# Loading a recurrent state by 32 by 32 blocks and finishing its transpose on VectorE

## The chip, the cores and the metric

The kernel runs on one core of a Trainium2 chip. The metric is the device time of one execution in microseconds (us). The program is unrolled: there is no loop on the chip, and each engine works through its own list of instructions in order. The engines are PE (TensorE), DVE (VectorE), ACT (ScalarE), POOL (GpSimd) and SP (SyncE, which here only issues DMAs); DMAs run on 16 DMA engines that all queues share.

## The reference

One layer of a hybrid decoder serves one prompt of 256 tokens and eight samples of eight tokens each, 320 tokens in all, in fp32. A combined projection feeds two recurrent branches. The branch that matters here is RWKV-7, with 16 heads of 64 by 64 state, indexed [value, key]:

```python
def step(s, inp):
    r_t, w_t, k_t, v_t, kk_t, a_t = inp
    sa = jnp.einsum('nhvk,nhk->nhv', s, kk_t)
    s = (s * w_t[:, :, None, :]
         - sa[..., None] * (kk_t * a_t)[:, :, None, :]
         + v_t[..., None] * k_t[:, :, None, :])
    return s, jnp.einsum('nhvk,nhk->nhv', s, r_t)
```

The prompt starts from a zero state. Each sample starts from a given state, `state_rwkv` (layers, samples, heads, value, key), and returns the new one. Both products with the old state sum over the key. The other branch, HGRN2, has eight heads and a state indexed [key, value]. After both, three more projections and a final norm follow.

## The kernel before

**Stages.** A start (to about 27 us) normalizes and transposes the tokens. Then a recorded part, to about 650 us, computes the projection in column blocks of 128 and both recurrences, for eight head pairs p of the RWKV branch (two heads at a time) beside the eight heads of the other. The last part, to the end, does the remaining projections. Weights come in blocks of 512 KB (`raw`); ScalarE rounds each to `whi`, VectorE subtracts to get the rest `wlo`, and TensorE multiplies both parts with the tokens (`hhi`, `hlo`) into `mps`. There are three buffers each of `raw`, `whi` and `wlo`.

**The recorder.** In the recorded part every call goes through `Recorder` (line 79): `V`, `S`, `G`, `T` and `Y` are proxies of VectorE, ScalarE, GpSimd, TensorE and SP. `add` (line 97) notes each operation with a cost and its tiles; a DMA on SP costs 380 ns and lands 5500 ns later in this plan, or 4500 to 6500 through scratch memory (line 169). `link` finds the dependencies and gives each operation a rank, the length of the longest chain behind it. `order` then simulates the engines and writes out the order in which each gets its instructions. `choose` (line 338) picks the next operation of an engine among those that can start within `AHEAD` = 300 ns of the earliest; `worth` (line 377) ranks them. On SP, an operation that belongs to no weight block has worth 3, a weight load whose block TensorE needs within 4500 ns has 2, and any other weight load 0. Nothing is reordered after that: an instruction that has to wait holds up everything behind it on its engine. In the profile all operations that are emitted this way carry line 199.

**The head pair.** `rwkv(p, ...)` (line 912) does one head pair. It asks for the two small matrices `w2a2` and for the samples' states of its two heads, in one DMA, as `s0` (line 923): 128 partitions (head, value) by 8 samples by 64 keys, 256 KB. The products with the old state need the key on the partitions. So four TensorE transposes with the identity turn `s0`, two samples at a time, into a PSUM bank `ps0`, and one ScalarE copy brings that to SBUF as `s0t` (lines 990 to 995): partition 64 x (sample mod 2) + key, then the sample's pair, then (head, value). `s0t` has one buffer. It is read by the matmuls with `az` (line 1140), which are part of a group that TensorE does side by side with the other branch's work, and by those with `rz` (line 1262), near the end of the head pair. `s0` itself is scaled and added to in place (line 1223), and stored as the new state (line 1241); it too has one buffer, so the next head pair's load waits for that store.

`at(name, shape)` gives a tile from a ring of `bufs` buffers (one unless told otherwise); `aps(name)` borrows one of six PSUM banks; `quads` are the four groups of 32 partitions. In the profile's names trailing digits are left out, so `s0` and the other branch's state of the same name are both `s`, and PSUM tiles of the recorded part are `bank`; `bank<-ident,s` are the four transposes of `s0`.

Of the kernel before, what the change touches and what calls it, by code (L numbers as in the profile page):

```python
# [20 lines left out]
NSEQ = 8  # L21
# [27 lines left out]

class Op:  # L50
    __slots__ = ("eng", "fn", "args", "kw", "cost", "lat", "uses", "mode", "passes", "cols", "stream",
                 "loans", "succ", "npred", "ready", "rank", "block", "margin", "wait", "port", "hold", "dma", "n", "group")


def span_of(ap):
# [23 lines left out]
class Recorder:  # L79
# [17 lines left out]
    def add(self, eng, name, fn, args, kw):  # L97
        o = Op()
        a, k = args, kw
        o.eng, o.fn, o.args, o.kw, o.n = eng, fn, args, kw, len(self.ops)  # L100
        aps = [x for x in (*args, *kw.values()) if hasattr(x, "start_partition") or hasattr(x, "tensor")]
        out = aps[0]
# [4 lines left out]
        for j, x in enumerate(aps):  # L107
            t_ = x.tensor
            if t_.name.startswith("bank"):
                n, off = divmod(x.offset, LOAN)  # L110
# [6 lines left out]
            o.uses.append((*self.spans[key], j == 0, "PSUM" in str(x.space)))  # L117
        o.lat = self.LAT[eng]
        o.dma = "dma" in name
        o.mode = None  # L120
        o.block, o.group = self.block, self.group
        o.margin, o.wait = 0, self.wait
# [4 lines left out]
        if eng == "PE":  # L127
# [4 lines left out]
            n = 1  # L132
# [39 lines left out]
        if eng in self.DRAIN and not o.dma:  # L172
            o.cost += self.SPARE
            if name == "tensor_reduce":
                n = 1
# [79 lines left out]
    def order(self):  # L255
# [4 lines left out]
        ready = {e: [] for e in self.real}  # L260
# [5 lines left out]
        port = {"V": 0.0, "G": 0.0}  # L266
        bigs = [o for o in self.ops if o.eng == "PE" and o.stream]
        at = {}
# [48 lines left out]
        def entry(q, now):  # L317

            at_, asking = {}, {}
            for o in q:  # L320
                want = wanted(o)
                if not want:
                    at_[o] = o.ready
                elif not asked[min(needs[want[0]])]:
                    asking.setdefault(min(want), []).append(o)
            room, rooms = len(idle), sorted(idle)
            for some in sorted(asking.values(), key=lambda s_: max((o.rank, -o.n) for o in s_), reverse=True):
                n = len(wanted(some[0]))
                first = min(o.ready for o in some)
                if first > now + self.SOON:  # L330
                    continue
                if n <= room:
                    for o in some:
                        at_[o] = max(o.ready, rooms[n - 1][0] + o.margin)
                room -= n
            return at_

        def choose(e):

            q = ready[e]  # L340
            now = free[e]
            if e == "PE":
                at_ = entry(q, now) or entry(q, 1e9)
                q = list(at_)
                if not q:
                    return None
                t_ = max(now, min(at_[o] for o in q))
            elif e in port:
                held = port["G" if e == "V" else "V"] - self.OVER
                if e == "V" and held > now and port["G"] == free["G"]:  # L350

                    held += min((o.cost for o in ready["G"] if o.hold and o.ready <= free["G"] - 40), default=0.0)
                at_ = {o: max(now, o.ready, held if o.port else 0.0) for o in q}
                t_ = min(at_.values())
            else:
                t_ = max(now, min(o.ready for o in q))
            if e == "PE":
                can = [o for o in q if at_[o] <= t_ + 1]
                own = [o for o in can if o.mode == mode and not o.stream]
                part = [o for o in can if o.mode != (128, 128)]  # L360
                if mode != (128, 128):
                    near = [o for o in q if o.mode == mode and at_[o] <= t_ + 60]
                    pool = own or near or part or can
                elif own:
                    pool = own
                elif part and (run_ >= self.APART and any(t_ - o.ready >= o.wait for o in part) or len(part) == len(can)):
                    pool = part
                else:
                    pool = [o for o in can if o.stream]
                o = max(pool, key=lambda o: (o.rank, -o.n))  # L370
                if o.stream:
                    o = min((o for o in pool if o.stream), key=lambda o: o.n)
                return max(t_, at_[o]), o
            if e not in port:
                at_ = {o: max(now, o.ready) for o in q}

            def worth(o):
                if o.block is None:
                    return (3 if e == "Y" else 1), o.rank
                slack = (at[o.block] - gone) * 147 + max(0, free["PE"] - t_)  # L380
                return (2 if slack < 4500 else 0), -o.n
            best = max((o for o in q if at_[o] <= t_ + self.AHEAD), key=worth)
            if at_[best] > t_ + 30:
                short = [o for o in q if at_[o] <= t_ + 30 and at_[o] + o.cost <= at_[best] + self.SLIP]
                if short:
                    best = max(short, key=worth)
            return t_, best

        while left:
            t_, o = min(filter(None, (choose(e) for e in ready if ready[e])), key=lambda x: (x[0], x[1].eng == "V"))  # L390
# [37 lines left out]
def hybrid_step(ctx, tc, x_prompt, x_sample, state_rwkv, state_hgrn, state_shift, norm_g, w_in,  # L428
# [4 lines left out]
    V, S, G, T = nc.vector, nc.scalar, nc.gpsimd, nc.tensor  # L433
# [14 lines left out]
    def ctile(shape, name, dt=F32, pool=rconst):  # L448
        return pool.tile(shape, dt, name=name, tag=name)

    ident = ctile([128, 128], "ident", pool=const)
# [57 lines left out]
    with tc.tile_pool(name="start", bufs=1) as st, \  # L509
# [160 lines left out]
        with tc.manual_schedule(engines={mybir.EngineType.PE, mybir.EngineType.Activation, mybir.EngineType.DVE,  # L670
# [15 lines left out]
            for c_ in range(4):  # L686
                ps = pst.tile([128, 512], F32, name="gps", tag="t")
# [96 lines left out]
            ps = pst.tile([128, 512], F32, name="cps", tag="t")  # L784
            T.transpose(ps[:, :128], rows, ident)
            V.tensor_copy(cols, ps[:, :106])
            ps = pst.tile([128, 512], F32, name="sps", tag="t")
# [44 lines left out]
    def ring(pool, tag, shape, bufs, dt, size, clear=False):  # L832

        if (pool.name, tag) not in rings:
            n_ = size or math.prod(shape[1:])
            if tag in SHARED:
                rings[pool.name, tag] = [0, [wide_[:, SHARED[tag]:SHARED[tag] + n_]]]
                if clear:
                    G.memset(wide_[:, 384:], 0.0)
        if (pool.name, tag) not in rings:  # L840
            rings[pool.name, tag] = [0, [pool.tile([128, n_], dt, name=f"{tag}_{j}", tag=f"{tag}_{j}")
                                         for j in range(bufs)]]
            for t_ in rings[pool.name, tag][1]:
                if clear:
                    G.memset(t_ if dt == F32 else t_.bitcast(F32), 0.0)
        r_ = rings[pool.name, tag]
        t_ = r_[1][r_[0] % len(r_[1])]
        r_[0] += 1
        t_ = t_[:shape[0], :math.prod(shape[1:])]
        if len(shape) == 2:  # L850
            return t_
        names = "abcdef"[:len(shape) - 1]
        return t_.rearrange(f"p ({' '.join(names)}) -> p {' '.join(names)}", **dict(zip(names, shape[1:])))
# [7 lines left out]
    def at(name, shape=(128, NT), tag=None, bufs=1, dt=F32):  # L861
        tag = tag or name
        return ring(pa, tag, list(shape), bufs, dt, SIZES.get(tag), tag in CLEAR)
# [5 lines left out]
    def aps(name="aps"):  # L869
        book.loans += 1  # L870
        at_ = lent[0]
        return bass.AP(at_.tensor, at_.offset + book.loans * LOAN, [list(d_) for d_ in at_.ap])
# [39 lines left out]
    def rwkv(p, r, k, v, za):  # L912
        c = lambda base: cols[:, base + p:base + p + 1]
# [7 lines left out]
            V.tensor_sub(dst[other], w2a2[own], dst[own].bitcast(F32))  # L921
        s0 = at("s0", (128, NSEQ, 64))
        Y.dma_start(s0, state_rwkv[0, :, 2 * p:2 * p + 2].rearrange("s h v k -> (h v) s k"))

        kk = at("kk", (128, 3, 128), tag="uK").rearrange("p a b -> p (a b)")[:, :NT]
        S.activation(kk, k, AF.Copy, scale=c(KK_))
# [6 lines left out]
        s = at("s", tag="uS")  # L933
# [4 lines left out]
        a = at("a", tag="uA")  # L938
# [11 lines left out]
        e = at("e", (128, 16))  # L950
# [37 lines left out]
        V.tensor_mul(blocks[:, :, 1:3], b64(e2), b64(a))  # L988
        V.tensor_mul(bk2[:, 0, 1], e2[:, NP_:], a[:, NP_:])
        s0t = at("s0t", (128, 4, 128))  # L990
        ps = aps("ps0")
        for sp in range(4):
            T.transpose(ps[:, 128 * sp:128 * sp + 128],
                        s0[:, 2 * sp:2 * sp + 2].rearrange("p s k -> p (s k)"), ident)
        S.copy(s0t.rearrange("p a b -> p (a b)"), ps)
        bon = at("bon")
        V.scalar_tensor_tensor(bon, r, c(RK), a, op0=ALU.mult, op1=ALU.mult)

# [79 lines left out]
        for d_ in range(1, 4):  # L1078
            n, m = 4 - d_, 8 * d_
# [28 lines left out]
        ps = aps("pP")  # L1108
# [5 lines left out]
        ps = aps("pD")  # L1114
# [154 lines left out]
        ps = aps("pyc")  # L1269
# [7 lines left out]
        sp = yh, yl  # L1277
# [3 lines left out]
        ps = aps("pvar")  # L1281
# [208 lines left out]
    quads = [slice(32 * q_, 32 * q_ + 32) for q_ in range(4)]  # L1490
# [91 lines left out]
    with tc.manual_schedule():  # L1582
# [4 lines left out]
        V, S, G, T, Y = (book.proxy(e) for e in ("V", "S", "G", "PE", "Y"))  # L1587
        record_all()
        V, S, G, T = real
# [29 lines left out]
    for m in range(KT):  # L1619
# [7 lines left out]
        ps = psf.tile([128, 512], F32, name="ppa", tag="f")  # L1627
# [3 lines left out]
        ps = psf.tile([128, 512], F32, name="ppb", tag="f")  # L1631
# [175 lines left out]
```

## Time and profile before

| | |
|---|---|
| Median of 3 runs | 1070.43 us (1070.11 to 1072.08) |
| The profiled execution | 1070.57 us |
| Its span, first to last instruction | 1068.6 us |
| Mean granted TensorE clock | 0.998 |
| Recorded part | about 27 to 650 us of the span |
| DMA over the span | 178.77 MB in 356369 packets, 167 GB/s |

How to read the profile: "busy" is the time in which an engine had an instruction in work, without register, semaphore and DMA-issuing instructions. Matmuls overlap in TensorE's pipeline, so a matmul's length is not what it costs; the distance between starts is. The idle time of an engine before an instruction is put down to what released it. "PEld" is TensorE's loading of weights, "SPq" the queue that issues DMAs. The rows that the argument uses stand in the prediction.

### The profile page before, as it was taken

What the parts mean: (1) busy time and instruction counts of PE and PEld (TensorE: products, weight loads), DVE (VectorE), ACT (ScalarE), POOL (GpSimd) and SP (SyncE); (2) the same over time, 40 slices, a digit from 0 to 9 for tenths busy, and PEclk for the clock granted to TensorE, in tenths of its full rate; (3) what the DMA queues carried; (4) which work ended last, traced back from release to release, by engine and by line L of the source; (5) the groups of instructions that cost most, each with busy time, mean ns of one, the idle gap of its engine ahead of it and who ended that gap; (6) DMA issues with size and microseconds to landing.
All of it is one profiled execution on the core that took longest, in us unless ns stands there. A gap on an engine that the chain in (4) does not pass through costs nothing.

```text
span 1068.6 us, 22991 instructions
## 1 busy us (share of the span) xinstructions
PE 1047.8 (98%) x8740; PEld 1011.1 (95%) x8740; DVE 758.5 (71%) x1608; ACT 696.9 (65%) x1616; POOL 124.1 (12%) x358
## 2 busy tenths in 40 slices
PE   7999999999999999999999999999999999999996
PEld 6999999999999999999999999999999999988886
DVE  8779889988988999989898856544443444446632
ACT  7757888878868878689688698444444444444412
POOL 9511201101111212011112000000000000000000
PEclk9999999999999999999999999999999999999999
DMA  6776585684774864866856837555455554587402
GB/s 203 195 178 180 131 210 139 157 225 122 185 195 120 210 188 119 203 162 158 210 131 178 214 110 206 168 158 164 142 154 150 147 157 143 155 295 245 169 20 98
DMA packets 356369, 178.77 MB, mean 167 GB/s; under 512 B 82013, under 2 KB 345440, under 8 KB 355684
## 3 DMA queue, kind: packets, MB, share of 16 engines
q1 hardware_dynamic: 355892, 176.01, 60.4%
q8 instruction: 68, 1.11, 0.4%
q10 hardware_dynamic: 368, 1.31, 0.3%
q14 instruction: 41, 0.34, 0.1%
HBM read 159.97 MB, written 17.32 MB: 166 GB/s over the span
## 4 chain that ended last, share of the span: by engine, by line
PE 87%; ACT 4%; DVE 4%; DMA 4%; issue 1%; SPq 0%; DVEq 0%; ACTq 0%
PE mps L199 39%; PE bank L199 10%; PE mps L494 5%; PE mps L493 5%; PE mps L492 5%; PE po L1678 3%; PE po L1679 3%; PE po L1680 3%; PE ppa L493 2%; PE ppb L494 2%; PE ppa L494 2%; PE ppb L493 2%; PE ppb L492 2%; PE ppa L492 2%; PE po L1684 1%; PE po L1683 1%
## 5 line engine op out<-in xcount | busy, mean ns | idle before, releaser
L199 PE MATMUL mps<-hhi,whi 128*128 128x320 f32 x1136 | 356.3, 314 | 0.0
L199 PE MATMUL mps<-hhi,wlo 128*128 128x320 f32 x1136 | 355.3, 313 | 0.4 <-DVE wlo L199 0.4
L199 PE MATMUL mps<-hlo,whi 128*128 128x320 f32 x1136 | 355.5, 313 | 0.0
L199 PEld LDWEIGHTS mps<-hhi,wlo 128*128 128x128 f32 x1136 | 213.6, 188 | 2.6 <-issue 1.5
L199 PEld LDWEIGHTS mps<-hlo,whi 128*128 128x128 f32 x1136 | 213.6, 188 | 2.4 <-issue 1.2
L199 PEld LDWEIGHTS mps<-hhi,whi 128*128 128x128 f32 x1136 | 213.7, 188 | 0.9 <-issue 0.4
L199 DVE TENSOR_TENSOR wlo<-raw,whi 128x1024 fp32r<-128x1024 f32 x140 | 171.5, 1225 | 24.9 <-ACT whi L199 23.6
L482 ACT CAST whi<-raw 128x1024 fp32r<-128x1024 f32 x82 | 85.7, 1048 | 146.5 <-PE mps L493 90.4
L483 DVE TENSOR_TENSOR wlo<-raw,whi 128x1024 fp32r<-128x1024 f32 x82 | 100.3, 1225 | 111.6 <-ACT whi L482 111.5
L199 ACT CAST whi<-raw 128x1024 fp32r<-128x1024 f32 x140 | 145.9, 1043 | 47.3 <-DMA raw<-in_w_in_dram 22.4
L494 PE MATMUL mps<-hhi,wlo 128*128 128x320 f32 x400 | 123.7, 309 | 0.1
L493 PE MATMUL mps<-hlo,whi 128*128 128x320 f32 x400 | 123.6, 309 | 0.0
L492 PE MATMUL mps<-hhi,whi 128*128 128x320 f32 x400 | 123.6, 309 | 0.0
L494 PEld LDWEIGHTS mps<-hhi,wlo 128*128 128x128 f32 x400 | 75.1, 188 | 0.3 <-DVE wlo L483 0.3
L492 PEld LDWEIGHTS mps<-hhi,whi 128*128 128x128 f32 x400 | 75.1, 188 | 0.0
L493 PEld LDWEIGHTS mps<-hlo,whi 128*128 128x128 f32 x400 | 75.1, 188 | 0.0
L1667 DVE TENSOR_TENSOR wlo<-raw,whi 128x1024 fp32r<-128x1024 f32 x32 | 38.5, 1222 | 37.5 <-ACT whi L1666 33.0
L1666 ACT CAST whi<-raw 128x1024 fp32r<-128x1024 f32 x32 | 33.0, 1051 | 47.7 <-DMA raw<-in_w_out_dram 19.5
L1678 PE MATMUL po<-whi,mhi 128*128 128x512 f32 x128 | 50.0, 391 | 0.0
L1679 PE MATMUL po<-whi,mlo 128*128 128x512 f32 x128 | 50.0, 391 | 0.0
L1680 PE MATMUL po<-wlo,mhi 128*128 128x512 f32 x128 | 50.0, 391 | 0.0
L492 PE MATMUL ppa<-yah,whi 128*128 128x320 f32 x128 | 39.7, 310 | 1.0 <-ACT yah L1613 1.0
(413 smaller groups left out, 1986.8 us busy)
## 6 DMA issues: line engine op xcount, KB each, us to landing
raw<-in_w_in_dram SPq DMA_DIRECT2D x194, 512.0 KB
raw<-in_w_out_dram SPq DMA_DIRECT2D x32, 512.0 KB
raw<-in_proj_a_dram SPq DMA_DIRECT2D x16, 512.0 KB
raw<-in_proj_b_dram SPq DMA_DIRECT2D x16, 512.0 KB
s<-in_state_hgrn_dram SPq DMA_DIRECT2D x8, 512.0 KB
ww<-scr SPq DMA_DIRECT2D x8, 512.0 KB
out_dram<-s SPq DMA_DIRECT2D x8, 512.0 KB
scrt<-ww SPq DMA_DIRECT2D x32, 120.0 KB
```

The source lines that it names most:

```text
L199: o.fn(*(real(x) for x in o.args), **{k: real(x) for k, x in o.kw.items()})
L482: S.copy(hi[:, ks], raw[:, ks])
L483: sub.tensor_sub(lo[:, ks], raw[:, ks], hi[:, ks].bitcast(F32))
L492: T.matmul(dst, hi[:, q, :], xhi[:, k, :], start=(k == 0), stop=False)
L493: T.matmul(dst, hi[:, q, :], xlo[:, k, :], start=False, stop=False)
L494: T.matmul(dst, lo[:, q, :], xhi[:, k, :], start=False, stop=(k == nk - 1))
L1666: S.copy(hi, raw)
L1667: V.tensor_sub(lo, raw, hi.bitcast(F32))
L1678: T.matmul(pt, h, hi, start=first, stop=False)
L1679: T.matmul(pt, l, hi, start=False, stop=False)
L1680: T.matmul(pt, h, lo, start=False, stop=end)
L1683: T.matmul(pt, h, hi, start=first, stop=False)
```

## The change

A second copy of the samples' states is loaded. For each sample and each half of the keys one DMA fetches the two heads' states as four blocks of 32 values by 32 keys: the 32 values go to the partitions, four blocks lie side by side, and each run of 32 keys (128 B) stays contiguous. Sixteen such DMAs of 16 KB per head pair put every block where the transposed block belongs in `s0t`, each block still untransposed. One VectorE transpose, which turns each 32 by 32 block in place, then writes `s0t`. The four TensorE transposes, their PSUM bank and the ScalarE copy are gone. `s0` is still loaded as before, for the state's update.

In the planner, DMAs whose target is `s0b` are marked `early` and have worth -1 on SP: they are issued only when no other DMA can start within the 300 ns.

```diff
     __slots__ = (...
-                 "loans", "succ", "npred", "ready", "rank", "block", "margin", "wait", "port", "hold", "dma", "n", "group")
+                 "loans", "succ", "npred", "ready", "rank", "block", "margin", "wait", "port", "hold", "dma", "n", "group", "early")
...
         o.dma = "dma" in name
+        o.early = o.dma and out.tensor.name.startswith("s0b")
...
                 if o.block is None:
-                    return (3 if e == "Y" else 1), o.rank
+                    return (-1 if o.early else 3 if e == "Y" else 1), o.rank
...
         s0 = at("s0", (128, NSEQ, 64))
         Y.dma_start(s0, state_rwkv[0, :, 2 * p:2 * p + 2].rearrange("s h v k -> (h v) s k"))
+        s0b = at("s0b", (128, 512))
+        for si in range(NSEQ):
+            for kh in range(2):
+                Y.dma_start(s0b[quads[2 * (si % 2) + kh], 128 * (si // 2):128 * (si // 2) + 128].rearrange("p (b c) -> p b c", c=32),
+                            state_rwkv[0, si, 2 * p:2 * p + 2, :, 32 * kh:32 * kh + 32].rearrange("h (x i) k -> i (h x) k", i=32))
...
         s0t = at("s0t", (128, 4, 128))
-        ps = aps("ps0")
-        for sp in range(4):
-            T.transpose(ps[:, 128 * sp:128 * sp + 128],
-                        s0[:, 2 * sp:2 * sp + 2].rearrange("p s k -> p (s k)"), ident)
-        S.copy(s0t.rearrange("p a b -> p (a b)"), ps)
+        V.transpose(s0t.rearrange("p a b -> p (a b)"), s0b)
```

## The prediction, made before the changed kernel ran

> **What bounds the kernel now.** I read the page's busy table and chain first, then a table of the loop over the eight head pairs (27 to 650 us), then the change's own rows. The page:
>
> ```profile
> span 1068.6 us, 22991 instructions
> ...
> PE 1047.8 (98%) x8740; PEld 1011.1 (95%) x8740; DVE 758.5 (71%) x1608; ACT 696.9 (65%) x1616; POOL 124.1 (12%) x358
> ...
> PE 87%; ACT 4%; DVE 4%; DMA 4%; issue 1%; SPq 0%; DVEq 0%; ACTq 0%
> ```
>
> Busy time by stretch; after the window and its length stand PE, PEld, DVE, ACT and POOL, then the granted clock, the DMA share and GB/s:
>
> ```profile
> 27.00:650.00 623.00, 618.33 (x6084) 604.40 (x6083) 539.23 (x1310) 497.14 (x1310) 99.64 (x305) 1.00 0.67 171
> 392.00:465.00 73.00, 72.23 (x729) 70.55 (x728) 66.80 (x169) 58.84 (x159) 11.31 (x36) 1.00 0.69 173
> ```
>
> TensorE is busy 99% of the loop at full clock (618.33 of 623), so what leaves TensorE's stream shortens the loop unless something else is late. VectorE is next: 87% over the loop (539.23), 92% in the fullest head pair shown (66.80 of 73). It has little room, and the change gives it work.
>
> **What goes, and what it is worth.** The groups of the lines view (busy us, mean ns of one | idle before, releaser):
>
> ```profile
> L199 PE MATMUL bank<-ident,s 128*128 128x128 f32 x32 | 5.3, 277 | 1.9 <-DMA s<-in_state_rwkv_dram 1.9
> ...
> L199 PEld LDWEIGHTS bank<-ident,s 128*128 128x128 f32 x32 | 3.8, 141 | 2.7 <-DMA s<-in_state_rwkv_dram 2.7
> ...
> L199 ACT COPY s0t<-bank 128x512 f32<-128x512 f32 x8 | 4.6, 579 | 4.0 <-PE bank L199 4.0
> ...
> L199 DVE STREAM_TRANSPOSE ww<-bk 128x640 f32<-128x640 f32 x8 | 6.7, 842 | 0.2
> ...
> L199 DVE STREAM_TRANSPOSE ww<-v 128x320 f32<-128x320 f32 x8 | 4.0, 496 | 0.2
> ```
>
> All 32 transposes go (four in each of eight head pairs), and so do eight ScalarE copies. The 277 ns is a pipelined length; the price comes from starts, in the timeline of TensorE:
>
> ```profile
> 364.63 0.31 PE L199 MATMUL bank<-fd,jr_cent 128*128 128x320 f32 x1
> 364.78 0.60 PE L199 MATMUL bank<-ident,s 128*128 128x128 f32 x4
> 365.13 0.39 PE L199 MATMUL mps<-hhi,wlo 128*128 128x320 f32 x1
> 365.36 0.31 PE L199 MATMUL mps<-hhi,whi 128*128 128x320 f32 x1
> ...
> 441.48 0.39 PE L199 MATMUL mps<-hhi,wlo 128*128 128x320 f32 x1
> 442.64 0.66 PE L199 MATMUL bank<-ident,s 128*128 128x128 f32 x4 [0.77 <-DMA s<-in_state_rwkv_dram]
> ```
>
> A matmul of 320 columns starts about 0.15 us after the one before (364.63 to 364.78, 365.36 after its slowed predecessor). From 364.63 to 365.36 is 0.73 us for two such matmuls and the four transposes: 0.73 - 2 x 0.15 = 0.43 us for four. **Eight times 0.43 is 3.4 us.**
>
> By the Trainium skill (TensorE: Matmul & The Clock Gate, Part 4: PE-mode transpose) one such transpose took about 275 ns in a kernel's context, mostly access latency. The length in the trace agrees (277 ns), the spacing does not: priced at 275 ns the 32 would be worth an estimated 8.8 us.
>
> The second gain is a wait. At 442.64 TensorE's queue stands for the state's DMA: 1.16 us between starts instead of 0.15. The weight-load row adds three such waits to **2.7 us**. In the changed kernel TensorE no longer touches the state tile, and the new blocks are asked for a whole head pair ahead: their buffer comes free with the previous head pair's VectorE transpose. The remaining 256 KB load of `s0` is needed only for the update at the end of the head pair. What is late next there is the weight supply; its rows follow:
>
> ```profile
> ACT whi L199 <- DMA raw<-in_w_in_dram: 22.4, 13, 3.8
> ...
> PEld bank L199 <- DMA s<-in_state_rwkv_dram: 2.7, 3, 1.0
> PEld bank L199 <- ACT rhs L199: 2.3, 4, 0.9
> PEld bank L199 <- DVE es L199: 0.7, 2, 0.4
> PEld mps L199 <- DVE wlo L199: 0.7, 1, 0.7
> ```
>
> ScalarE waits 13 times for a weight block's transfer, up to 3.8 us, yet the weight loads lose only 0.7 us to a late `wlo`: the splits run far enough ahead to soak up delays of that size. So I keep the whole 2.7, with 0 as its other end.
>
> **What comes.** One VectorE transpose of 128x512. Between 496 ns at 320 columns and 842 ns at 640 that is 496 + 192/320 x 346 = 704 ns, eight times 5.6 us. VectorE has 539 of 623 us filled, and queued behind each transpose are the splits `wlo` that TensorE waits for; the 0.7 us row above says the splits have lead. I cost it at 0; without that lead it is at most 5.6. ScalarE's 4.6 us and 4.0 us of waiting go: also 0, at best the 2.3 us that TensorE loses to ScalarE's `rhs` copies. The transpose's waits are for its DMAs (a head pair old) and for the last readers of the old `s0t`, the wait that the copy had: 0.
>
> Sixteen DMAs per head pair, 128 in all, each 128 pieces of 128 B. Their issue time on SP, by the same kind of small transfer (min/median/max ns):
>
> ```profile
> L199 SPq DMA_DIRECT2D scr<-big x32: 326/430/1716, 63.8 to 574.9; - x32
> L199 SPq DMA_DIRECT2D scri<-w x32: 382/482/2034, 91.1 to 588.4; - x32
> L199 SPq DMA_DIRECT2D uQ<-scr x32: 417/426/928, 95.6 to 607.3; - x32
> ```
>
> At 430 ns, 16 take 6.9 us of SP's queue per head pair, 55 us in all. The planner counts 380 ns (line 169), so a full burst ends 16 x 0.05 = 0.8 us later than planned. The diff gives them the last place whenever another DMA is nearly ready. SP stands in many waits for buffers, so they should fall into gaps. Queued behind them on SP are weight loads and the scratch round trips; those wait at most for one issue, 0.4 us, where the planner's clock is right. On the DMA engines the nearest row is the window 414.4 to 417 us, which holds almost only 128 B pieces:
>
> ```profile
> DMA packets 1749, 0.23 MB, mean 88 GB/s; under 512 B 1748, under 2 KB 1748, under 8 KB 1748
> ## 3 DMA queue, kind: packets, MB, share of 16 engines
> q1 hardware_dynamic: 1748, 0.22, 55.5%
> ```
>
> 0.555 x 2.6 us x 16 engines / 1748 = 13 ns a piece. The new 2048 pieces per head pair are 2048 x 13 / 16 = 1.7 us of all engines: 2% of a head pair whose share is 0.69. I cost that at 0, except at the start, where there is no room:
>
> ```profile
> 31.00:33.00 2.00, 2.00 (x16) 2.00 (x15) 1.97 (x5) 1.22 (x3) 1.49 (x6) 1.00 1.11 289
> 33.00:35.00 2.00, 2.00 (x17) 2.00 (x16) 1.52 (x4) 1.79 (x5) 1.13 (x5) 1.00 1.12 303
> 35.00:37.00 2.00, 1.97 (x15) 1.71 (x13) 1.90 (x6) 1.89 (x7) 1.18 (x8) 1.00 1.21 291
> ```
>
> From 31 to 37 us the engines are full (shares above 1), as the first states and weight blocks come in. The first head pair's 16 transfers join that queue, and a weight block behind them is 1.7 us later. I take all **1.7 us as lost once**; bounds 0 and 6.9 (the SP burst in one piece).
>
> **Sum**, against the profiled execution's 1070.57 us (its span 1068.6 and 2.0 around it): 1070.6 - 3.4 - 2.7 + 1.7 = 1066.2, which I give as **1066 us**. That execution lies 0.1 above the median of the runs, 1070.43.
>
> **Rivals.**
>
> *The wait comes back (chance 0.21).* The gain in work stays, but the loop's end is set by what follows: the splits on a fuller VectorE or the weight transfers. Then 3.4 goes, the 2.7 reappears as waits for `wlo`, and the start costs its 1.7: 1070.6 - 3.4 + 1.7 = 1068.9; with half of VectorE's 5.6 us unhidden, 1071.7. For it: VectorE at 92% in a head pair. Against it: TensorE's 0.7 us row.
>
> *SP becomes the bound: slower (0.19).* If a burst lies in one piece ahead of a weight load, the load is 6.9 us late; 3.8 was soaked up, 3.1 reaches TensorE. It decides from the ninth issue in a row on (9 x 0.43 = 3.9), and from the second head pair on it outweighs the gain: 2 x 3.1 = 6.2 against 4.4. With three head pairs it is 1066.2 + 9.3 = 1075.5, with all eight 1091. For it: a transfer on SP stood up to 2034 ns in its issue, so the price is not fixed. Against it: the last place and the lead of a head pair.
>
> In the Trainium skill (DMA: Bandwidth & Descriptors, Rules for kernel authors) many small transfers should be coalesced, since under 64 KB one pays mostly overhead. These are 16 KB each: the trace agrees, with 430 ns of issue against 1.7 us / 16 = 0.1 us of engine time; this is the rival's case.
>
> *Each transpose is worth its length (0.05).* If the 277 ns were the price, 32 x 0.277 = 8.9 goes: 1070.6 - 8.9 - 2.7 + 1.7 = 1060.7. The starts at 364.78 and 365.13 speak against it.
>
> **How the numbers follow.** The forecast has 0.55, its own range 1062.2 (both gains, no start cost, ScalarE's 2.3 as well) to 1068.4. A difference of 0.2%, 2.1 us, is about what a measurement can tell from none. Faster: 0.55 and the 0.05; a part of the first rival falls under 1068.3 as well, a part of the forecast near its edge falls out, so 0.60. Same: 0.21. Slower: 0.19. The range goes from the forecast's low end, 1062.2, to 1075, which takes in the first rival and two head pairs of the second; left out are most of three and more (0.12) and the long transposes (0.05).
>
> **What would show it.** Right: no `bank<-ident,s` group and no TensorE wait for the state; a transpose of 128x512 of about 704 ns eight times, landing requests in SP's gaps; TensorE's busy time in the loop down by some 3 to 4 us. Wrong: new waits of TensorE for `wlo`, ScalarE's waits for weight transfers well above 22.4 us, or SP issues of the new blocks in runs of nine and more just ahead of a weight load. The order of the whole loop is planned anew, so small waits will move about; a shift of some 2 us either way from that alone would blur the terms.

## The result, and the profile after

| | before | changed |
|---|---|---|
| Median, four runs each side by side | 1070.96 us (1070.11 to 1072.08) | 1099.45 us (1097.15 to 1105.18) |
| Profiled execution | 1070.57 us | 1098.85 us |
| Its span | 1068.6 us | 1096.7 us |
| Mean granted TensorE clock | 0.998 | 0.989 |

The changed kernel is slower by 28.5 us: the ratio is 1.0267, 95% interval 1.0247 to 1.0287. The forecast was 1066 us, with a range from 1062.2 to 1075. The page of the changed kernel (span; busy time, share and instructions of each engine; shares of the chain that ended last):

```profile
span 1096.7 us, 23064 instructions
...
PE 1056.1 (96%) x8708; PEld 1015.0 (93%) x8708; DVE 764.7 (70%) x1616; ACT 694.1 (63%) x1608; POOL 122.5 (11%) x358
...
PE 78%; DVE 7%; DMA 6%; ACT 4%; POOL 2%; issue 2%; SPq 1%; DVEq 0%; ACTq 0%; POOLq 0%
```

TensorE has 32 matmuls fewer, as planned, yet its share of the chain falls from 87% to 78%: something else now often ends last. Busy time by stretch from 27 to 690 us (columns as in the prediction), first after, then before:

```profile
27.00:690.00 663.00, 637.41 (x6118) 618.49 (x6118) 551.50 (x1324) 501.79 (x1313) 97.92 (x305) 0.99 0.66 168
```

```profile
27.00:690.00 663.00, 656.86 (x6341) 642.18 (x6340) 563.25 (x1340) 519.89 (x1345) 99.64 (x305) 1.00 0.67 172
```

TensorE stands idle for 25.6 us after (663 - 637.41) and for 6.1 before. So 19.5 us of the loss are new stalls, and the clock, 0.99 in place of 1.00, is a second part. No engine is fuller than before: the change made a queue late, not an engine busy.

The operation itself came out as worked out. In the groups of the changed kernel (busy us, mean ns | idle before):

```profile
L200 DVE STREAM_TRANSPOSE s0t<-s0b 128x512 f32<-128x512 f32 x8 | 5.6, 704 | 0.0
```

704 ns, eight times, and VectorE never waits for the blocks. The waits tell where the time went (engine and tile that waited, what for: total us, times, longest). Changed kernel:

```profile
ACT whi L200 <- DMA raw<-in_w_in_dram: 47.9, 20, 4.6
POOL ww L200 <- DMA ww<-scr: 37.7, 4, 18.4
...
PEld mps L200 <- DVE wlo L200: 6.7, 10, 2.3
PEld bank L200 <- DVE rl L200: 5.8, 4, 2.3
...
PEld bank L200 <- POOL fd L200: 5.0, 3, 4.6
```

The same wait of GpSimd in the kernel before:

```profile
POOL ww L199 <- DMA ww<-scr: 10.9, 3, 4.0
```

ScalarE's wait for weight blocks went from 22.4 to 47.9 us and GpSimd's for a scratch round trip from 10.9 to 37.7, in one case 18.4 us. TensorE now waits for `wlo`, 6.7 us in place of 0.7, and for tiles of the recurrences (`rl`, `fd`). The two largest waits are for DMAs that SP issues. In the timeline of SP (start, us, instruction, how many) of the changed kernel, around that longest wait:

```profile
209.02 1.05 SPq L200 DMA_DIRECT2D s0b<-in_state_rwkv_dram  x2
210.12 0.43 SPq L200 DMA_DIRECT2D raw<-in_w_in_dram  x1
210.59 2.00 SPq L200 DMA_DIRECT2D s0b<-in_state_rwkv_dram  x4
...
218.00 2.91 SPq L200 DMA_DIRECT2D s0b<-in_state_rwkv_dram  x4
220.95 0.55 SPq L200 DMA_DIRECT2D ww<-scrs  x1
221.54 0.59 SPq L200 DMA_DIRECT2D s0b<-in_state_rwkv_dram  x1
222.23 1.80 SPq L200 DMA_DIRECT2D scr<-big  x4
...
225.80 0.54 SPq L200 DMA_DIRECT2D raw<-in_w_in_dram  x1
226.51 0.54 SPq L200 DMA_DIRECT2D ww<-scr  x1
```

From 209.02 to 227.05 us SP issues 30 DMAs, 16 of them for `s0b`, without a pause: 0.60 us each, where the planner counts 0.38. If the plan has these 30 without a pause as well, SP is 30 x 0.22 = 6.6 us behind it after the last. The same round trip before:

```profile
209.02 1.77 SPq L199 DMA_DIRECT2D scr<-big  x4
210.88 0.63 SPq L199 DMA_DIRECT2D scrs<-dns  x1
211.61 0.91 SPq L199 DMA_DIRECT2D out_dram<-s  x1
212.61 0.61 SPq L199 DMA_DIRECT2D uv<-scrt  x1
213.31 1.03 SPq L199 DMA_DIRECT2D raw<-in_w_in_dram  x1
214.51 0.62 SPq L199 DMA_DIRECT2D ww<-scr  x1
215.18 0.59 SPq L199 DMA_DIRECT2D ww<-scrs  x1
```

Here nine DMAs take 6.16 us, from 209.02 to 215.18: 0.68 each. So the price was there before the change as well; SP only had room for it. After, the read of scratch is issued 12 us later. (The order was planned anew, so not all of the 12 us is delay.) Who waits for it shows the timeline of GpSimd and then that of TensorE, changed kernel:

```profile
216.27 0.62 POOL L200 TENSOR_TENSOR fd<-id,fq 128x256 fp32r<-128x256 f32 x1 [4.06 <-PE bank L200]
235.31 0.17 POOL L200 MEMSET ww<- 128x40 f32 x1 [18.43 <-DMA ww<-scr]
235.43 1.49 POOL L200 TENSOR_TENSOR fd<-id,fq 128x256 fp32r<-128x256 f32 x1
```

```profile
232.33 0.31 PE L200 MATMUL mps<-hhi,whi 128*128 128x320 f32 x1
236.97 0.51 PE L200 MATMUL bank<-fd,jr_sum 128*128 128x256 f32 x1 [4.33 <-POOL fd L200]
237.27 0.47 PE L200 MATMUL mps<-hlo,whi 128*128 128x320 f32 x1
237.54 0.47 PE L200 MATMUL mps<-hhi,wlo 128*128 128x320 f32 x1
```

Read from the TensorE rows back: TensorE stands 4.33 us for GpSimd's `fd`. That instruction is queued behind a memset of the tile `ww`, which waits 18.43 us for the scratch read that SP issued at 226.51, in among 512 KB loads. Of these 18.43 us, 9.6 pass before the read is issued (216.89 to 226.51) and 8.8 after it. The weight matmuls behind it start without a further wait; they only came after it on the list. After the stall the matmuls start 0.27 us apart (237.27 to 237.54) in place of 0.15: the clock is halved for 3.5 us, as the windows of the changed kernel show (the third figure from the end is the granted clock):

```profile
232.00:237.00 5.00, 0.67 (x6) 0.40 (x4) 1.85 (x5) 1.37 (x2) 1.60 (x2) 1.00 1.12 241
237.00:240.50 3.50, 3.50 (x14) 3.50 (x15) 1.20 (x5) 2.92 (x7) 0.00 (x0) 0.51 0.84 223
240.50:244.00 3.50, 3.50 (x25) 3.50 (x25) 3.22 (x9) 0.97 (x3) 0.00 (x0) 1.00 1.08 260
```

Five such stretches lie in the recorded part after, none before; at half speed 3.4 us lose 1.7, so 8.5 together. With 19.5 of stalls and 3.4 of work that left, 19.5 + 8.5 - 3.4 = 24.6 of the 28.1 us of span are accounted for.

### The profile page after: what moved, and what is told of

Same layout as the page of the kernel before. It is cut to its first block, busy times and chain, and to the rows that moved or that the text cites. A ratio compares the mean times of both kernels' runs of the same rounds, so it can differ in the third digit from the quotient of the medians.

```text
span 1096.7 us, 23064 instructions
## 1 busy us (share of the span) xinstructions
PE 1056.1 (96%) x8708; PEld 1015.0 (93%) x8708; DVE 764.7 (70%) x1616; ACT 694.1 (63%) x1608; POOL 122.5 (11%) x358
## 4 chain that ended last, share of the span: by engine, by line
PE 78%; DVE 7%; DMA 6%; ACT 4%; POOL 2%; issue 2%; SPq 1%; DVEq 0%; ACTq 0%; POOLq 0%
PE mps L200 32%; PE bank L200 9%; PE mps L494 5%; PE mps L493 5%; PE mps L495 5%; DVE wlo L200 3%; PE po L1681 3%; PE po L1680 3%; PE po L1682 3%; DMA raw<-in_w_in_dram 2%; PE ppa L494 2%; PE ppb L494 2%; PE ppb L493 2%; PE ppb L495 2%; PE ppa L495 2%; PE ppa L493 2%
## 5 line engine op out<-in xcount | busy, mean ns | idle before, releaser
L200 PE MATMUL mps<-hhi,wlo 128*128 128x320 f32 x1136 | 360.6, 317 | 4.2 <-DVE wlo L200 4.2
L200 PEld LDWEIGHTS mps<-hhi,wlo 128*128 128x128 f32 x1136 | 216.6, 191 | 8.9 <-DVE wlo L200 6.7
L200 ACT CAST whi<-raw 128x1024 fp32r<-128x1024 f32 x140 | 145.8, 1044 | 73.9 <-DMA raw<-in_w_in_dram 47.9
L495 PE MATMUL mps<-hhi,wlo 128*128 128x320 f32 x400 | 123.6, 309 | 0.0
L495 PEld LDWEIGHTS mps<-hhi,wlo 128*128 128x128 f32 x400 | 75.1, 188 | 0.0
```

Source lines behind the costliest of these rows:

```text
L200: o.fn(*(real(x) for x in o.args), **{k: real(x) for k, x in o.kw.items()})
L495: T.matmul(dst, lo[:, q, :], xhi[:, k, :], start=False, stop=(k == nk - 1))
```

## The experiments

**Theory:** the 128 issues on SP put it behind the planner's clock, and the planned order turns that into stalls on other engines. **Rivals:** the bytes and pieces on the DMA engines; the transposes on a full VectorE; the new order itself, whatever it loads. Each ratio is to runs of the kernel before on the same chip at the same time, whose median moved between 1070.96 and 1073.74 us, so ratios are compared, not times.

| run | what it is | median us | ratio (95% interval) |
|---|---|---|---|
| first_only | changed, loads of the first head pair only | 1079.40 | 1.0058 (1.0038 to 1.0078) |
| loads_only | before, with the loads and a tiny reader | 1091.37 | 1.0155 (1.0115 to 1.0195) |
| sp600 | changed, planner counts 600 ns per DMA | 1074.38 | 1.0011 (0.9993 to 1.0030) |
| before_sp600 | before, the same planner | 1071.05 | 0.9975 (0.9961 to 0.9989) |
| no_loads | changed, same order, no block loads | 1075.91 | 1.0024 (1.0009 to 1.0039) |
| four_of_sixteen | changed, a quarter of the loads | 1083.68 | 1.0103 (1.0086 to 1.0120) |
| quarter_size | changed, all loads, a quarter of the bytes | 1103.84 | 1.0291 (1.0275 to 1.0306) |
| gpsimd_queue | changed, loads issued by GpSimd | 1075.07 | 1.0019 (1.0003 to 1.0034) |
| gpsimd_sp600 | the same, planner counts 600 ns | 1073.14 | 1.0019 (1.0010 to 1.0029) |
| before_minus | before's order, transposes and copy out | 1065.96 | 0.9950 (0.9939 to 0.9962) |
| before_swap | the same, VectorE's transpose in | 1069.10 | 0.9955 (0.9941 to 0.9968) |
| planned_without_loads | changed, planner knows no loads | 1072.64 | 1.0010 (0.9999 to 1.0021) |
| two_state_buffers | before, two buffers of `s0` | 1070.38 | 0.9987 (0.9978 to 0.9997) |
| two_buffers_sp600 | the same, planner counts 600 ns | 1077.69 | 1.0034 (1.0019 to 1.0049) |
| block_loads_spread | whole change in before's order, every third SP DMA | 1092.90 | 1.0179 (1.0158 to 1.0200) |
| block_loads_spread_gpsimd | the same from GpSimd | 1077.59 | 1.0037 (1.0023 to 1.0050) |
| block_loads_early | as block_loads_spread, every second SP DMA | 1077.72 | 1.0035 (1.0022 to 1.0049) |
| block_loads_early_gpsimd | the same from GpSimd | 1072.96 | 0.9990 (0.9976 to 1.0005) |

### The loads, or what they replace

`first_only` emits the changed kernel's order, but only the first head pair's loads:

```diff
+        seen = 0
...
-            book.emit(o)
+            seen += o.early
+            if not o.early or seen <= 16:
+                book.emit(o)
```

> The changed kernel with its order of instructions on every engine, but the sixteen block loads are issued for the first head pair only; the later seven transposes turn the first pair's blocks, so the samples' RWKV results of those pairs are not the reference's. Theory A (the 112 other issues hold up what stands behind them on SP): the loss goes, 1064 to 1071 us, and TensorE's waits for wlo, yz, fd and rl shrink to what they were before. Theory B (planning anew without the four TensorE transposes gave an order that is bad in itself): stays within 6 us of the changed kernel, 1093 to 1105. Theory C (VectorE's eight transposes of 704 ns are what is late): the same as B, 1093 to 1105.

`loads_only` keeps everything of before and adds the loads, in the last place as in the change, with a VectorE copy of 16 columns as their reader:

```diff
+        V.tensor_copy(at("s0d", (128, 16)), s0b[:, 0:512:32])
```

> The kernel before, its TensorE transposes kept, with the sixteen block loads per head pair beside them (same last place on SP) and a 128x16 VectorE copy, some 0.2 us, where the VectorE transpose would stand, so that each pair's loads follow the last one's reader. Theory A: the loads alone make it slow, 1090 to 1110 us. Theories B and C: the loads cost little, 1070 to 1077.

Without 112 of the loads the loss shrinks from 2.67% to 0.58%, which is 1079.40 us and above the 1071 that was expected at most; with the loads and nothing removed it is 1.55%. So most of the loss is the loads, and neither VectorE's transposes nor the missing TensorE work. `loads_only` isn't clean: it still has TensorE's wait for `s`, which grew, since that load too is issued by SP (weight loads of TensorE, waits):

```profile
PEld bank L200 <- DMA s<-in_state_rwkv_dram: 6.0, 4, 3.0
```

### The planner's price

`sp600` changes one number of the changed kernel's planner; `before_sp600` is the same in the kernel before, as a control:

```diff
-            o.cost, o.lat = 380, 5500
+            o.cost, o.lat = 600, 5500
```

> The changed kernel, with one number of the planner changed: a DMA on SP is counted as 600 ns instead of 380, near what 29 of them in a row took (209.0 to 227.1 us of the changed kernel's trace). Theory A: the planner leaves the room that SP needs, and a large part of the 28 us comes back: 1066 to 1085 us. Theory B or C: some other order of the same quality, 1090 to 1105.

> The control of the run before it: the kernel before with 600 ns for a DMA on SP. All theories: little to gain, since SP has 16 DMAs per head pair fewer, 1066 to 1074 us. If it gains as much as the changed kernel does, the price of 380 ns is a fault of its own and says nothing of the change.

The same instructions, 128 loads on SP among them, now cost 1.0011 in place of 1.0267. The windows of `sp600`, 172 to 245 us:

```profile
172.00:245.00 73.00, 72.69 (x732) 71.27 (x731) 65.73 (x164) 58.79 (x160) 10.40 (x36) 1.00 0.69 168
```

TensorE is busy 72.69 of 73 us; in the changed kernel the same window has

```profile
172.00:245.00 73.00, 68.36 (x687) 66.49 (x687) 58.92 (x147) 55.96 (x151) 13.46 (x36) 0.98 0.65 162
```

The control gained a little too, 0.25%, so against its own control the change still loses 0.36%. That SP's issues are dear isn't the whole cause, then: in another order the same issues cost almost nothing. This fits an order that was made for a cheaper SP. It does not show that only a truer price gives a good order: `block_loads_early`, further down, has 128 issues on SP in an order that was planned with 380 ns and comes to 1.0035.

### Issues or bytes

`no_loads` emits none of the loads, in the changed kernel's order; `four_of_sixteen` every fourth from the second head pair on; `quarter_size` all of them, one of the four blocks of each. Their edits, in that order:

```diff
-            book.emit(o)
+            if not o.early:
+                book.emit(o)
```

```diff
+            if not o.early or seen <= 16 or seen % 4 == 0:
```

```diff
+            if o.early and seen > 16:
+                o.args = [x[:, 0:1] for x in o.args]
```

> The changed kernel's order of instructions without any of the 128 block loads; the block tile is set to zero once, so the samples' products with the old RWKV state are left out. What is left against the kernel before: no TensorE transposes, no wait for the state, eight VectorE transposes, and the new order. If the rest of the forecast held (3.4 and 2.7 us), 1064 to 1068 us. If the eight VectorE transposes or the order that the planner made for them cost something of their own, 1070 to 1077, as the run with the first pair's loads alone (6 us slower than before) leaves open; then that run's first burst cost at most 3 us.

> The changed kernel's order, sixteen loads for the first head pair, and from the second pair on every fourth of them only (4 DMAs and 64 KB instead of 16 and 256 KB; the samples' RWKV results are not the reference's). With the next run it parts issues from bytes: both move the same bytes. If the number of issues is the price, 1081 to 1087 us (6 us, and a quarter of the 20 us between this order with and without the later loads).

> The changed kernel with all sixteen issues per head pair, each from the second pair on fetching one block of four (32 pieces of 128 B instead of 128; the samples' RWKV results are not the reference's). If the number of issues on SP is the price: as slow as the changed kernel, 1093 to 1102 us. If the pieces on the DMA engines are the price: as the run before, 1081 to 1087.

The issues of `s0b` (min/median/max ns) and ScalarE's wait for weight blocks, in `four_of_sixteen` and then in `quarter_size`:

```profile
L200 SPq DMA_DIRECT2D s0b<-in_state_rwkv_dram x44: 334/570/1538, 32.4 to 522.3; - x44
...
ACT whi L200 <- DMA raw<-in_w_in_dram: 39.5, 19, 5.1
```

```profile
L200 SPq DMA_DIRECT2D s0b<-in_state_rwkv_dram x128: 311/421/1797, 32.1 to 542.6; - x128
...
ACT whi L200 <- DMA raw<-in_w_in_dram: 60.4, 23, 6.4
```

After the first head pair both move the same bytes, one in 28 DMAs and one in 112. The one with the 112 is as slow as the changed kernel and a little more (1.0291; its 1103.84 us are 2 us above what was expected at most), the other has lost most of it (1.0103). Bytes and pieces are ruled out; the price goes with the number of DMAs on SP. No run parts the issue itself from another fixed cost that a DMA may have in SP's queue. In this order, from none to 128, it is (1.0267 - 1.0024) x 1071 = 26 us, or 0.20 us per issue. From none to 44 it is 8.5 us, 0.19 per issue. That is near the 0.22 us by which one DMA exceeds the planner's count, but it holds for this order alone, as the last pair of runs shows.

### Another queue

`gpsimd_queue` lets GpSimd issue the loads; `gpsimd_sp600` is that with the 600 ns:

```diff
-                Y.dma_start(s0b[...
+                G.dma_start(s0b[...
```

> The changed kernel with the 128 block loads issued by GpSimd instead of SP; the planner counts 950 ns and 4500 ns to landing for them there. GpSimd is busy 12% of the span. If SP's issue time is the whole price, it is as good as the changed order without the loads, 1064 to 1076 us. If GpSimd now holds up its own work (fd, which TensorE waits for), 1080 or more.

> The changed kernel with the block loads issued by GpSimd and a DMA on SP counted as 600 ns: both repairs together. SP then has the number of DMAs that it had before. If they add up, it is faster than before with the same count (0.9975 of before), by some part of the 6.1 us: 0.992 to 0.998 of before. If VectorE or GpSimd is late, 0.998 to 1.004.

Off SP the loss falls to 0.19%, though each issue costs GpSimd 551 ns (tile row of `gpsimd_queue`):

```profile
L200 POOL DMA_DIRECT2D s0b<-in_state_rwkv_dram x128: 551/551/730, 29.4 to 526.6; - x128
```

Counting 600 ns on SP adds nothing here: 1.0019 both times, in an order in which SP has no more to issue than before.

### The gain, in an order that stays

A list planned anew moves everything, so these take before's order and take things out of it as it is emitted. `before_minus` leaves out the four transposes and the copy; `before_swap` puts VectorE's transpose of a tile of zeros in the copy's place. `planned_without_loads` is the changed kernel without the 16 `dma_start`, so that the planner doesn't see them.

```diff
+        gone = len(book.ops)
...
+        leave.update(range(gone, len(book.ops) - 1))
+        turn[len(book.ops) - 1] = p
...
-            book.emit(o)
+            if o.n in turn:
+                V.transpose(s0t, s0b)
+            elif o.n not in leave:
+                book.emit(o)
```

> The kernel before with its order of instructions, from which the 32 TensorE transposes and the eight ScalarE copies are left out and nothing is put in (the transposed state is set to zero once, so the samples' products with the old RWKV state are missing). This is the gain of the forecast alone, in an order that does not change. If the forecast's 3.4 us of transposes and 2.7 us of waits are real, 6.1 us below before: 1064 to 1066.5 on a chip where before is 1070.5 to 1073. If TensorE's time is set by other engines anyway, less than 2 us.

> The order of before without the TensorE transposes, and where each ScalarE copy stood a VectorE transpose of 128x512 of a tile that is set to zero once (so the samples' products with the old RWKV state are missing; no block loads). If VectorE's eight times 704 ns are hidden, as the prediction had it, the gain of the order of before stays: 0.993 to 0.997 of before. If they are what took it back in the orders planned anew: 0.998 to 1.003.

> The changed kernel without the block loads, as in the run without any, but the planner does not know of them either, so the order is made for what runs. If the 2.4 permille by which that run was slower than before came from room that the planner shared out for the loads, it goes, and the time is 1064 to 1069 us. If the eight VectorE transposes or the loss of lead between engines is the cause, it stays at 1071 to 1077.

In the old order the removal is worth 0.50%, 5.4 us, and VectorE's eight transposes cost no more than the uncertainty (0.9955 against 0.9950). With an order planned anew, nothing is left of it: 1.0010. So some 0.55%, 5.9 us, goes in replanning alone, before a single block is loaded.

`two_state_buffers` takes TensorE's wait for `s` away in another way; `two_buffers_sp600` adds the planner's 600 ns:

```diff
-        s0 = at("s0", (128, NSEQ, 64))
+        s0 = at("s0", (128, NSEQ, 64), bufs=2)
```

> The kernel before with two buffers for s0 and nothing else, so that the state of the next head pair is loaded without waiting for the store of the last. It is the forecast's second term alone, 2.7 us of TensorE's waits for the state: 0.1 to 0.3 percent faster than before if it stands alone, the same within 0.2 percent if the new order takes it back.

> The kernel before with two buffers for s0 and a DMA on SP counted as 600 ns, no block loads. If the two gains (0.9987 and 0.9975) add: 0.995 to 0.998 of before. If each is only a lucky order: 0.998 to 1.002.

One edit gained 0.13%, the other 0.25%, and both together lost 0.34%, outside both ranges of the expectation. Gains that come by way of the planned order do not add up here.

### The whole change in the old order

Last, all of the change in before's order: the loads are put between SP's DMAs as the list is emitted, one after every third in `block_loads_spread` (every second among the first 38) and after every second throughout in `block_loads_early`. The two `_gpsimd` runs put them at the same places of the list, on GpSimd.

```diff
+                if o.eng == "Y":
+                    past += 1
+                    if past % 2 == 0:
+                        for ab in coming:
+                            nc.sync.dma_start(*ab)
+                            break
```

> The whole change in the order of before: the TensorE transposes and ScalarE copies left out, the VectorE transpose at the copy's place (in the first head pair later, after 38 DMAs), and the block loads issued by SP one at a time, after every third DMA of the old order (every second in the first head pair). If bunches of loads are the harm: 0.994 to 1.003 of before. If SP has no room for 128 more issues wherever they stand: 1.008 to 1.03.

> The same with the block loads issued by GpSimd, one at a time at the same places of the order. SP then does what it did before. If SP's issues are the only price of the loads: as the run of the swap alone, within 0.3 percent of it. If GpSimd's issues hold up fd or the other work that TensorE waits for, 1.002 or more of before.

> As the spread loads on SP, but one after every second DMA of the old order, so that a head pair's sixteen are issued after 32 of its some 54 DMAs and VectorE should not wait for them. If the 1.8 percent of the run before came from VectorE's 16.5 us of waiting: 0.996 to 1.004 of before. If it came from SP's room: 1.010 to 1.025.

> The same with the loads issued by GpSimd. If SP's issues are the only price of the loads, and VectorE no longer waits for them: 0.995 to 0.999 of before, which would beat both kernels. If GpSimd's issues have a price of their own: 1.000 to 1.006.

The number of `block_loads_spread`, 1.0179, is the one that was expected if SP has no room, but its trace shows another cause. With every third place the last blocks came just before the transpose, and VectorE waited (waits of `block_loads_spread`; in the run from GpSimd it was 6.8 us):

```profile
DVE s0t L1607 <- DMA s0b<-in_state_rwkv_dram: 16.5, 4, 7.4
```

With earlier places that wait is gone. Against `before_swap`, which has all but the loads, SP's issues cost 1.0035 - 0.9955 = 0.80%, 8.6 us, and GpSimd's 0.35%, 3.8 us. Spread out, 128 issues on SP cost a third of the 26 us that they cost in the changed kernel's order, but still more than the 5.4 us that the change can gain. From GpSimd they leave 0.9990, which can't be told from no change.

Even these 8.6 us are not 128 equal parts. In the profiled executions most of them lie in one place. TensorE and the clock from 75 to 90.06 us, in `block_loads_early` and then in `block_loads_early_gpsimd`:

```profile
75.00:90.06 15.06, 11.06 (x56) 10.40 (x55) 8.46 (x22) 6.15 (x11) 0.17 (x1) 0.77 0.77 195
```

```profile
75.00:90.06 15.06, 14.36 (x98) 14.06 (x97) 11.36 (x28) 8.68 (x14) 4.52 (x9) 1.00 0.83 207
```

TensorE is busy 3.3 us less, and a mean clock of 0.77 over 15.06 us is worth another 3.5: 6.8 in all (`before_swap` has 14.36 us and 1.00 there too). Ahead of it SP issues the scratch read `bk` at 73.37 us instead of 70.09, with seven block loads among the DMAs since 61 us. ScalarE waits 5.08 us for that read, and TensorE then 3.64 us for the `whi` that stands behind it on ScalarE's list.

No version with the block loads beats the kernel before by more than its uncertainty. Of the runs that compute everything, the one that gains most is before itself with 600 ns in its planner, 0.9975.

## Why the prediction was wrong, point by point

**The step that failed** is the one on SP's issues: "a full burst ends 16 x 0.05 = 0.8 us later than planned", "they should fall into gaps", and what is queued behind them waits "at most for one issue, 0.4 us, where the planner's clock is right". It was costed at 0; in the same order, with and without the loads, it is 26 us (`no_loads` against the changed kernel), 22.4 of them by the 112 loads after the first head pair. Two things were wrong with it.

The first is the price. I took the median length of an issue, 430 ns, from rows of small transfers. The new issues have just that median in the changed kernel (first row), but 577 ns in `block_loads_early` (second row), where each stands alone among other DMAs:

```profile
L200 SPq DMA_DIRECT2D s0b<-in_state_rwkv_dram x128: 312/432/2006, 31.1 to 536.3; - x128
```

```profile
L1615 SPq DMA_DIRECT2D s0b<-in_state_rwkv_dram x128: 317/577/1900, 27.9 to 565.6; - x128
```

In the changed kernel's trace, too, the 89 block loads issued next after another block load have a median of 430 ns, the 39 after another kind of DMA 578. With these, the long cases and what lies between, one DMA takes 0.60 us in a stretch without pauses. Nine DMAs in a row of the kernel before give 0.68. The excess over the planner's 380 ns is then 0.22 us or more, not 0.05, and 16 of them are 3.5 us, not 0.8.

The second is "where the planner's clock is right". The last place guards against a late DMA only if the planner knows when the DMA is due. Its worth of -1 puts the loads into gaps of the plan; the chip has smaller gaps, since everything else on SP is underpriced too. A slip then isn't one issue long. It stays in SP's queue until SP next waits for something anyway, and in the meantime weight loads and scratch round trips, and the engines behind them, are late. `sp600` bears this out: with the same 128 issues, planned at a truer price, it has 1.0011, and `planned_without_loads`, which has none, 1.0010.

**The rival that SP becomes the bound** had the right side and the right engine; it was given 0.19. Its mechanism was another, and its top of 1091 too low. It asked for nine issues in a row ahead of a weight load. The changed kernel has one such run of nine in the whole loop, with a scratch write and no weight load behind it, and 16 loads in 18 us mixed with other DMAs do the same harm. It priced only the weights; the larger single stalls came by way of scratch and GpSimd.

**The gain** was right as a sum: 6.1 us against 5.4 measured (interval 4.1 to 6.5) with the order held; no run holds the order and parts its two terms. **VectorE at 0** agrees: 0.05% between `before_minus` and `before_swap`, with an uncertainty of 0.2%. **DMA pieces at 0** was right: with a quarter of the bytes the kernel is no faster. **The start at 1.7 us** (0 to 6.9) lies within its bounds at twice the size: from `no_loads` to `first_only` it is 0.34%, 3.6 us, with an uncertainty of 2.7 us. Whether the pieces cost it, as forecast, or the issues, no run tells. No run tried **ScalarE's relief** by itself.

**The order planned anew** was allowed "some 2 us either way"; it costs 5.9 us in `planned_without_loads` and 7.4 in `no_loads`, both against `before_swap`. In parts of 0.1% of before the whole adds up as -5.0 (removal), +0.5 (VectorE), +6.9 (order), +3.4 (first loads), +20.9 (the other 112 loads) = 26.7, each known to about 2 of these parts.

**What stays open:** why the orders planned anew lose the gain. It may be chance, as the two edits that do not add up suggest, or something in the way the list is made; no run tells these apart. Fewer and larger loads weren't tried either.

## What to carry to other kernels

Price a DMA's issue from a stretch of the issuing queue without pauses (time over count), not from the median length of one, and compare that with what the planner counts: an error that was harmless with few DMAs is multiplied by every one added. A last place in a plan does not protect the rest of a queue whose plan counts too little per issue; ask for each added issue who is queued behind it on that queue, and who waits for those. Where a list is planned anew, test a gain of half a per cent with the order held, because the new order alone can take it away.

## What the runs showed of the hardware

A stall of TensorE can cost more than its length: the clock may halve after it, and for shorter stalls than the 4.33 us one. Two stalls in the timeline of TensorE, changed kernel:

```profile
48.15 0.42 PE L200 MATMUL bank<-rh,jr_sum 128*128 128x320 f32 x1 [1.80 <-ACT rh L200]
...
494.24 0.71 PE L200 MATMUL bank<-yz,uE 128*128 128x128 f32 x4 [2.28 <-ACT yz L200]
```

After the 1.80 us the granted clock was 0.52 for 3.5 us, after the longer 2.28 us it stayed at 1.00:

```profile
45.94:49.35 3.41, 1.61 (x10) 1.24 (x9) 2.61 (x4) 3.05 (x5) 0.76 (x3) 1.00 0.98 266
49.40:52.90 3.50, 3.50 (x16) 3.50 (x15) 3.31 (x8) 1.18 (x3) 0.79 (x5) 0.52 0.61 165
...
489.67:493.08 3.41, 2.29 (x16) 2.02 (x14) 3.20 (x9) 3.33 (x10) 0.84 (x1) 1.00 0.81 231
493.08:496.49 3.41, 2.25 (x15) 2.05 (x16) 3.41 (x12) 3.30 (x9) 1.16 (x4) 1.00 0.52 156
496.49:499.90 3.41, 3.41 (x151) 3.18 (x150) 3.34 (x15) 3.00 (x12) 0.23 (x2) 1.00 0.56 161
```

The difference is where a stall lies. In the trace's clock records the five slow stretches begin at 49.35, 168.82, 237.08, 414.58 and 557.94 us; the later four lie 35, 55, 107 and 149 times 3.413 us behind the first, so they follow one grid. Laid on that grid, the 1.80 us fall into one window (3.41 - 1.61 idle), while the 2.28 us are cut by a boundary at 493.08 into 1.12 and 1.16. The windows ahead of the five slow stretches have 1.70, 1.80, 2.07, 2.46 and 3.30 us of idle TensorE. The two idlest windows of this execution that no slow stretch follows have 1.72 and 1.46. So in this trace about half a window of idleness is enough; a sharp limit can't be read from it.

The Trainium skill (TensorE: Matmul & The Clock Gate, Part 1: The HAM clock gate) gives half rate after an idle window of about 3.4 us, in windows that run freely. The windows and their length agree with the 3.413 us; that a whole window must be idle does not, with the 1.80 us beside it.

The second thing is that an issue on GpSimd, with 551 ns hardly cheaper than the 577 on SP, cost this kernel less than half (3.8 against 8.6 us at the same places of the list, most of the 8.6, in the profiled execution, in one late scratch read and the stall after it). What counted was who else stood in the queue.
